# Weight tiles moved by 64 bytes in SBUF, to a multiple of 128 bytes, in a hybrid convolution and RWKV-7 block

## The chip, the cores and the metric

The kernel runs on one core of one Trainium2 chip. The metric is the device time of one execution in microseconds; the time shown is the median of three runs. A difference of 0.2% (some 6 us) is about what a measurement of this kernel can tell from no change.

## What is computed

One decoder block for 2,048 tokens and 1,024 channels, all in fp32. With `h = rmsnorm(x)·(1 + scale) + shift` the reference does, cut to what matters:

```python
p = jnp.einsum('bsd,de->bse', h, w_in[l])          # 1024 -> 73 tiles of 128 channels
c_val, c_gate, c_og, ts, r_og, g_conv, g_rwkv = jnp.split(p, SPLITS, axis=-1)
y_conv = _conv_branch(c_val, c_gate, c_og, ..., w_conv_out[l])   # depthwise conv 31, layernorm, swish, @ w_conv_out
y_rwkv = _rwkv7_branch(ts, r_og, ..., w_rwkv_out[l])             # delta-rule recurrence over time, @ w_rwkv_out
m = jax.nn.sigmoid(g_conv) * y_conv + jax.nn.sigmoid(g_rwkv) * y_rwkv
x = x + gate[:, None, :] * jnp.einsum('bsd,de->bse', m, w_out[l])
return _rmsnorm(x, final_g)
```

The four large products (`w_in`, `w_conv_out`, `w_rwkv_out`, `w_out`) hold nearly all of the arithmetic.

## The kernel before

**Products in three parts.** Each fp32 operand is split into a high part (type fp32r) and the rest, `hi` and `lo`, and a product is the sum of three: hi·hi, lo·hi, hi·lo. For `w_in` the weights are the stationary operand and the activations `h_hi`, `h_lo` the moving one. The tokens are worked off in four blocks of 512 (`TB`); a block's 512 columns are sent as two halves of 256 (`MS = 2`), and each half is a weight load and a matmul of its own:

```python
# L200-207, mm3k: one of the eight k of a product
for t, (ww, aa) in enumerate(((whi, ahi), (whi, alo), (wlo, ahi))):
    for q in range(ms):
        qs = slice(q * NS, q * NS + NS)
        nc.tensor.matmul(ps[:, qs], ww[:, k, :], aa[k][:, qs], ...)      # L206
```

So one product is 8·3·2 = 48 pairs of a weight load of 128 columns and a matmul of 256 columns.

**Two phases.** Phase 1 does, block by block, the 73 products with `w_in` (L206 with `h_hi`, `h_lo`), the convolution on VectorE (L774, one instruction for each of 30 further taps), and the recurrence in chunks of 64 tokens (L534 to L739). Phase 2 does the products with `w_rwkv_out` and `w_conv_out` (L206 with `MS2 = 1`, so matmuls of 512 columns; moving operands `o_*`, `u_*`, `m_*`) and with `w_out` (L1090 to L1092). In the last the roles are swapped: `m_hi`, `m_lo` (under the names `o_*` in blocks 0 and 2, `m_*` in blocks 1 and 3) are stationary and the weights move, 256 columns at a time.

**Weight tiles.** They come from one pool, `whl`, with seven slots (`WB = 7`) of 128 partitions by 4,096 bytes. `load_w` fetches a raw tile into a slot (`w_st`), ScalarE rounds it into a second (`w_hi`, L189), GpSimd or VectorE subtracts into a third (`w_lo`, L191), and for `w_in` both are written to DRAM, so that blocks 1 to 3 fetch the two halves ready made (L183, L186). All DMAs are issued in order by the SP queue; a load into a slot waits until the matmuls that read the slot's last tile are done. Two front products of block 0 keep their weights elsewhere, in tiles called `w_f`.

**Where tiles lie.** Pools opened without a side are stacked from the low end of SBUF, in the order in which they are opened: the constants `cst`, the weights `whl`, then `c1`, `l3`, `lt` (constants, state and chunk tiles of phase 1), in whose place phase 2 puts `b2` and `hl` (`y`, `u_*`, `m_*`). Pools opened with `side="right"` are stacked from the high end: `e1`, `xp`, `hp`, `e2` (among them `h_hi`, `h_lo`) and later `ob`, `f2`, `oa` (among them `o_*`). Each tile takes its bytes in a partition rounded up to 32. `cst` begins at byte 1,152 = 9·128 and holds

```
ident 512, v 580 -> 608, g_col 32, hgate_col 32, ghalf 64, shift_col 32, ones 512, hlg 32, hlb 32   = 1856 = 14*128 + 64
```

so the weight tiles begin at byte 3,008, and every one of the seven lies 64 bytes past a multiple of 128 (192 past a multiple of 256). Other places that matter below, as bytes past a multiple of 256: `h_*` 192, `o_*` 160, `m_*` and `u_*` 32, `w_f` 96, `th` and `yj` 128, `oc` and `vv` 96 or 224. From `xp`, `hp` and `e1` down to the smallest tile, what lies on the right is independent of the size of `cst`. Between the end of the left pools of phase 1 (byte 147,936) and the lowest tile that phase 2 opens on the right while these are still in use (`mr0`, byte 148,128) there are 192 bytes.

The instructions' order on each engine is worked out when the program is built, from a simulated timeline of the operations.

Of the kernel before, what the change touches and what calls it, by code (L numbers as in the profile page):

```python
# [9 lines left out]
F32 = mybir.dt.float32  # L10
# [8 lines left out]
P = 128  # L19
D = 1024  # L20
KT = D // P
# [60 lines left out]
def hybrid_block(ctx: ExitStack, tc: tile.TileContext, x, vecs, convk, w2a2, final_g, ada, w_in, w_co, w_ro, w_o, crow, out,  # L82
# [6 lines left out]
    cst = ctx.enter_context(tc.tile_pool(name="cst", bufs=1))  # L89
# [22 lines left out]
    def vc(name, j=None):  # L112
        o, w = VOFF[name]
        return v[:, o:o + w] if j is None else v[:, o + j:o + j + 1]
# [150 lines left out]
    nc.sync.dma_start(v, vecs)  # L265
    ab = vc("ada_b")
    hlg = cst.tile([P, KT], F32, name="hlg")
    hlb = cst.tile([P, KT], F32, name="hlb")
    nc.vector.tensor_scalar(out=hlg, in0=vc("conv_ln_g"), scalar1=0.5, scalar2=None, op0=ALU.mult)
    nc.vector.tensor_scalar(out=hlb, in0=vc("conv_ln_b"), scalar1=0.5, scalar2=None, op0=ALU.mult)  # L270

# [898 lines left out]
```

## Time and profile before

| | |
|---|---|
| time, median of 3 runs | 3031.91 us (3030.95 to 3034.19) |
| the profiled execution's own time | 3047.45 us |
| its span, first to last instruction | 3045.7 us |
| busy PE, weight loads (PEld), DVE, ACT, POOL | 96%, 90%, 68%, 31%, 41% |
| mean granted TensorE clock | 0.975 |
| moved by DMA | 699.24 MB, mean 230 GB/s |

The profile is one execution. PE is TensorE's matmuls, PEld its weight loads, DVE VectorE, ACT ScalarE, POOL GpSimd, SP the queue that issues the DMAs. A group of instructions is named by source line and by "out<-in" with the names of the tiles; for a matmul the first name behind the arrow is the moving operand and the second the stationary one. No view shows an address; the places above come from the allocation.

### The profile page before, as it was taken

What the parts mean: (1) busy time and instruction counts of PE and PEld (TensorE: products, weight loads), DVE (VectorE), ACT (ScalarE), POOL (GpSimd) and SP (SyncE); (2) the same over time, 40 slices, a digit from 0 to 9 for tenths busy, and PEclk for the clock granted to TensorE, in tenths of its full rate; (3) what the DMA queues carried; (4) which work ended last, traced back from release to release, by engine and by line L of the source; (5) the groups of instructions that cost most, each with busy time, mean ns of one, the idle gap of its engine ahead of it and who ended that gap; (6) DMA issues with size and microseconds to landing.
All of it is one profiled execution on the core that took longest, in us unless ns stands there. A gap on an engine that the chain in (4) does not pass through costs nothing.

```text
span 3045.7 us, 64763 instructions
## 1 busy us (share of the span) xinstructions
PE 2914.9 (96%) x25672; PEld 2735.9 (90%) x25672; DVE 2058.4 (68%) x3896; ACT 935.2 (31%) x1759; POOL 1250.1 (41%) x1786
## 2 busy tenths in 40 slices
PE   6999998999999999899999999999999999899998
PEld 6889998989989899899999999999999988788988
DVE  6587877686867676668676767676779635776433
ACT  4433434332323232233232323232323222333201
POOL 3455555434343425143434263625467204565000
PEclk9899999999999999999999999999999999999999
DMA  8666758564758578847474777655647778889674
GB/s 303 205 234 209 251 196 282 199 235 145 250 185 260 187 242 287 235 137 246 151 246 139 246 254 252 199 185 165 212 141 246 229 264 309 320 311 344 239 280 163
DMA packets 368673, 699.24 MB, mean 230 GB/s; under 512 B 136241, under 2 KB 154993, under 8 KB 368370
## 3 DMA queue, kind: packets, MB, share of 16 engines
q1 hardware_dynamic: 368370, 695.10, 68.0%
q8 instruction: 202, 3.31, 0.4%
q14 instruction: 101, 0.83, 0.1%
HBM read 506.14 MB, written 187.70 MB: 228 GB/s over the span
## 4 chain that ended last, share of the span: by engine, by line
PE 61%; DMA 16%; DVE 9%; POOL 7%; SPq 3%; issue 2%; ACT 2%; ACTq 0%; DVEq 0%; POOLq 0%
PE ps_main L206 43%; DMA w_st<-w_in_t 3%; PE aux L534 2%; POOL TT L627 2%; POOL itmp L625 2%; DMA w_st<-w_ro_t 2%; DMA w_st<-w_co_t 2%; PE pout L1091 2%; PE pout L1092 2%; PE pout L1090 2%; PE xo L689 2%; DVE acc L774 1%; DMA w_gr<-grow_d 1%; PE xo L684 1%; PE xo L695 1%
## 5 line engine op out<-in xcount | busy, mean ns | idle before, releaser
L206 PE MATMUL ps_main<-h_hi,w_hi 128*128 128x256 f32 x4608 | 971.3, 289 | 12.2 <-ACT w_hi L189 3.4
L206 PE MATMUL ps_main<-h_hi,w_lo 128*128 128x256 f32 x4608 | 965.4, 289 | 8.5 <-POOL w_lo L191 5.0
L206 PE MATMUL ps_main<-h_lo,w_hi 128*128 128x256 f32 x4608 | 971.3, 289 | 0.0
L206 PEld LDWEIGHTS ps_main<-h_hi,w_hi 128*128 128x128 f32 x4608 | 735.3, 194 | 24.1 <-ACT w_hi L189 3.9
L206 PEld LDWEIGHTS ps_main<-h_hi,w_lo 128*128 128x128 f32 x4608 | 731.8, 194 | 17.5 <-POOL w_lo L191 6.3
L206 PEld LDWEIGHTS ps_main<-h_lo,w_hi 128*128 128x128 f32 x4608 | 733.9, 194 | 8.1 <-issue 0.5
L774 DVE SCALAR_TENSOR_TENSOR acc<-u,ck,acc 128x512 f32<-128x512 f32 x928 | 698.6, 753 | 20.8
L625 POOL TENSOR_TENSOR itmp<-La,TT 128x126 f32<-128x126 f32 (+22 forms) x496 | 180.2, 363 | 140.9 <-DMA La<-dA 106.1
L627 POOL TENSOR_TENSOR TT<-TT,itmp 128x126 f32<-128x126 f32 (+22 forms) x496 | 188.2, 379 | 37.3
L681 ACT ACTIVATE Se<-S,pe 128x128 f32<-128x128 f32 x256 | 89.0, 395 | 239.4 <-DVE S L699 239.2
L191 POOL TENSOR_TENSOR w_lo<-w_st,w_hi 128x1024 fp32r<-128x1024 f32 x47 | 113.6, 2417 | 112.8 <-ACT w_hi L189 106.2
L699 DVE TENSOR_TENSOR S<-xo,Se 64x128 f32<-64x128 f32 x256 | 73.5, 287 | 104.1 <-PE xo L695 100.8
L189 ACT CAST w_hi<-w_st 128x1024 fp32r<-128x1024 f32 x71 | 74.2, 1046 | 182.4 <-DMA w_st<-w_in_t 147.4
L534 PE MATMUL aux<-KR,BK 64*128 64x128 f32 x1024 | 121.5, 307 | 7.4 <-POOL BK L517 4.1
L534 PEld LDWEIGHTS aux<-KR,BK 64*128 64x128 f32 x1024 | 104.2, 208 | 18.7 <-POOL BK L517 4.3
L562 POOL TENSOR_TENSOR BK<-BK,pe 128x1024 f32<-128x1024 f32 x32 | 62.0, 1939 | 140.7 <-PE aux L534 113.1
L691 DVE TENSOR_TENSOR uv<-xo,rn 64x256 f32<-64x256 f32 x128 | 53.8, 420 | 90.7 <-PE xo L689 88.8
L686 DVE TENSOR_TENSOR XO<-xo,XO 128x256 f32<-128x256 f32 x128 | 53.7, 420 | 89.9 <-PE xo L684 70.5
L537 DVE TENSOR_TENSOR As<-aux,maskA 128x512 f32<-128x512 f32 x128 | 83.8, 685 | 36.9 <-PE aux L534 35.6
L684 PE MATMUL xo<-S,KR 128*128 128x128 f32 x512 | 83.0, 285 | 15.0 <-DVE S L699 14.9
L786 ACT ACTIVATE th<-ps_main 128x512 f32<-128x512 f32 x64 | 38.1, 596 | 190.1 <-PE ps_main L206 168.9
L431 ACT ACTIVATE t<-ps_main,mu 128x512 f32<-128x512 f32 x96 | 65.6, 683 | 97.4 <-PE ps_main L206 90.4
(301 smaller groups left out, 5318.2 us busy)
## 6 DMA issues: line engine op xcount, KB each, us to landing
w_hi<-kh_in SPq DMA_DIRECT2D x219, 512.0 KB, 5.1
w_lo<-kl_in SPq DMA_DIRECT2D x219, 512.0 KB, 4.0
w_st<-w_in_t SPq DMA_DIRECT2D x73, 512.0 KB, 4.9
kh_in<-w_hi SPq DMA_DIRECT2D x71, 512.0 KB, 2.9
kl_in<-w_lo SPq DMA_DIRECT2D x71, 512.0 KB, 3.7
w_hi<-kh_ro SPq DMA_DIRECT2D x32, 512.0 KB, 5.6
w_lo<-kl_ro SPq DMA_DIRECT2D x32, 512.0 KB, 5.5
w_hi<-kh_co SPq DMA_DIRECT2D x32, 512.0 KB, 5.5
```

The costliest lines, as they stand in the source:

```text
L189: nc.scalar.copy(hi, st)
L191: lo_eng.tensor_tensor(out=lo, in0=st, in1=hi.bitcast(F32), op=ALU.subtract)
L206: nc.tensor.matmul(ps[:, qs], ww[:, k, :], aa[k][:, qs], start=(k == 0 and t == 0 and q == 0), stop=(k == KT - 1 and t == 2 and q == ms - ...
L431: nc.scalar.activation(t1, ps, AF.Identity, scale=mu1[:, mi:mi + 1])
L534: nc.tensor.matmul(pA[hh][:, c // 2, es], BK[hs, cc, es], KR[hs, cc, es], start=(c == 0), stop=(c == 3), skip_group_check=True)
L537: nc.vector.tensor_tensor(out=Asb[:, hh, c4 * 4:c4 * 4 + 4, :].rearrange("p (a e) n -> p a (e n)", e=2), in0=pA[hh], in1=flat(maskA).unsqu ...
L625: nc.gpsimd.tensor_tensor(out=tmp[:, :ni, :nt], in0=La[:, j:j + 1, j + 1:].broadcast_to([P, ni, nt]), in1=TT[:, :ni, j:j + 1].broadcast_to ...
L627: nc.gpsimd.tensor_tensor(out=TT[:, :ni, j + 1:], in0=TT[:, :ni, j + 1:], in1=tmp[:, :ni, :nt], op=ALU.add)
L681: nc.scalar.mul(Se[:, q, :], Sg[:, q, :], R[q]["pe"][:, c:c + 1])
L684: nc.tensor.matmul(xo[:, q, :], R[q]["KR"][:, cc, es], Sg[:, q, :], start=(q == 0), stop=(q == 1), skip_group_check=True)
L699: nc.vector.tensor_tensor(out=Sg[hs, :, hs], in0=xo[hs, 2:4, hs], in1=Se[hs, :, hs], op=ALU.add)
L774: nc.vector.scalar_tensor_tensor(out=acc if i + 1 < HALO else yj, in0=u[:, i:i + TB], scalar=ck[:, j, i:i + 1], in1=acc, op0=ALU.mult, op1 ...
```

## The change

```diff
     hlg = cst.tile([P, KT], F32, name="hlg")
-    hlb = cst.tile([P, KT], F32, name="hlb")
+    hlb = cst.tile([P, 24], F32, name="hlb")[:, :KT]
```

`hlb` (the halved bias of the convolution's layer norm) takes 96 bytes in a partition in place of 32; its first eight columns are used as before. `cst` is then 1,920 = 15·128 bytes, the weight tiles begin at byte 3,072 (a multiple of 128, 256 and 512), and everything stacked on them from the low end moves up by 64 bytes too. Nothing on the right moves. No instruction is added, removed or changed in its shape.

## The prediction

> **What bounds the kernel now.** I read the page's busy shares, slices and chain first, then the groups, then who waits for whom on PE and SP, and last the timeline, for the pace of the matmuls.
>
> ```profile
> span 3045.7 us, 64763 instructions
> PE 2914.9 (96%) x25672; PEld 2735.9 (90%) x25672; DVE 2058.4 (68%) x3896; ACT 935.2 (31%) x1759; POOL 1250.1 (41%) x1786
> ...
> PE   6999998999999999899999999999999999899998
> ...
> PE 61%; DMA 16%; DVE 9%; POOL 7%; SPq 3%; issue 2%; ACT 2%; ACTq 0%; DVEq 0%; POOLq 0%
> ...
> L206 PE MATMUL ps_main<-h_hi,w_hi 128*128 128x256 f32 x4608 | 971.3, 289 | 12.2 <-ACT w_hi L189 3.4
> L206 PE MATMUL ps_main<-h_hi,w_lo 128*128 128x256 f32 x4608 | 965.4, 289 | 8.5 <-POOL w_lo L191 5.0
> L206 PE MATMUL ps_main<-h_lo,w_hi 128*128 128x256 f32 x4608 | 971.3, 289 | 0.0
> L206 PEld LDWEIGHTS ps_main<-h_hi,w_hi 128*128 128x128 f32 x4608 | 735.3, 194 | 24.1 <-ACT w_hi L189 3.9
> ...
> L774 DVE SCALAR_TENSOR_TENSOR acc<-u,ck,acc 128x512 f32<-128x512 f32 x928 | 698.6, 753 | 20.8
> ...
> L191 POOL TENSOR_TENSOR w_lo<-w_st,w_hi 128x1024 fp32r<-128x1024 f32 x47 | 113.6, 2417 | 112.8 <-ACT w_hi L189 106.2
> ...
> L189 ACT CAST w_hi<-w_st 128x1024 fp32r<-128x1024 f32 x71 | 74.2, 1046 | 182.4 <-DMA w_st<-w_in_t 147.4
> ```
>
> PE is busy 96% of the span in almost every slice, and 61% of the chain is PE. In phase 1 alone there are 3 · 4,608 = 13,824 pairs of weight load and matmul. What others make PE wait for on account of weight tiles is small:
>
> ```profile
> PE ps_main L206 <- POOL w_lo L191: 5.0, 6, 1.4
> ...
> PE ps_main L206 <- DMA w_lo<-kl_in: 3.5, 3, 2.5
> ...
> PE ps_main L206 <- ACT w_hi L189: 3.4, 2, 2.3
> ...
> PE ps_main L206 <- DMA w_hi<-kh_in: 2.5, 1, 2.5
> ...
> PE pout L1091 <- DMA w_lo<-kl_o: 2.0, 1, 2.0
> ...
> SPq L183 <- PE ps_main L206: 717.8, 194, 10.8
> ```
>
> Loads of weights wait for PE to free a slot (717.8 us on SP), and PE hardly waits for loads (3.5 + 2.5 + 2.0 = 8.0 us). So the one price that decides is the pace of PE. A duration of 289 ns overlaps with the next, so the pace is read from counts in stretches of unbroken matmuls of 256 columns:
>
> ```profile
> 128.00:160.00 32.00, 32.00 (x269) 1.00 0.74 249
> ...
> 2856.00:2899.50 43.50, 43.50 (x375) 1.00 0.58 200
> 2718.00:2744.00 26.00, 26.00 (x221) 1.00 0.74 254
> ```
>
> The columns are the stretch, its length, PE's busy time with the count, the granted clock, the share of DMA. About two of each count only reach in over an edge. The first stretch is phase 1 (`h` moving, `w` stationary): 32.00 / 267 = 119.9 ns. The second is the last product of block 2 (`w` moving, `o` stationary): 43.50 / 373 = 116.6 ns. The third is that of block 1 (`w` moving, `m` stationary): 26.00 / 219 = 118.7 ns. With 120 ns, phase 1's pairs are 13,824 · 0.120 = 1,659 us, more than half of the span.
>
> **The change, part by part.** No instruction, DMA or wait is added or removed; addresses move. So there are only possible differences in the pace of what reads or writes the moved tiles.
>
> *PE, phase 1: weights stationary, from 64 to 0 past a multiple of 128.* The trace has a place where the same matmul takes its weights from elsewhere, the `w_f` tiles at 96 past a multiple of 256, next to rows of the ordinary slots at 192:
>
> ```profile
> 54.81 0.64 PE L206 MATMUL ps_f<-h_hi,w_f 128*128 128x256 f32 x4
> 55.29 0.40 PE L206 MATMUL ps_f<-h_lo,w_f 128*128 128x256 f32 x2
> 55.53 0.64 PE L206 MATMUL ps_f<-h_hi,w_f 128*128 128x256 f32 x4
> ...
> 128.07 0.40 PE L206 MATMUL ps_main<-h_hi,w_lo 128*128 128x256 f32 x2
> 128.31 0.40 PE L206 MATMUL ps_main<-h_hi,w_hi 128*128 128x256 f32 x2
> 128.55 0.40 PE L206 MATMUL ps_main<-h_lo,w_hi 128*128 128x256 f32 x2
> 128.79 0.40 PE L206 MATMUL ps_main<-h_hi,w_lo 128*128 128x256 f32 x2
> ```
>
> From 54.81 to 55.53 there are 4 + 2 matmuls in 0.72 us, 120 ns each; from 128.07 to 128.79 six in 0.72 us, 120 ns each. Weights that lie 96 bytes further back in their 256, not even on a multiple of 64, go at the same pace. That is the nearest row, and I take 0 from it. The ends: `m` against `o` as stationary operand are the same instructions with the same moving weights, and differ in where the operand lies (32 or 160 past a multiple of 256). They differ by 118.7 − 116.6 = 2.1 ns, so a place can cost that much. Upward I bound with 2.1 · 13,824 = +29 us. Downward the best pace that any 256-column matmul shows is 116.6 ns: (119.9 − 116.6) · 13,824 = −46 us.
>
> A rule of the Trainium skill bears on this: TensorE: Matmul & The Clock Gate, section "Step-by-step: what each phase is for", says that PE reads the moving and the stationary operand through two independent ports, and that loading the next weights takes no read bandwidth from the running matmul. By that rule a stationary operand's place could not matter and the sum would be 0; the 2.1 ns between `o` and `m` are not explained by it, so I keep both ends.
>
> *PE, phase 2.* In the products of 512 columns the weights are stationary too:
>
> ```profile
> 2804.75 50.40 PE ps_main L206 x216
> 2899.96 89.60 PE ps_main L206 x384
> ```
>
> 89.60 / 384 = 233.3 ns, just twice the 116.6 ns of the best 256-column rows, so nothing here is above the best pace; I take 0. In L1090 to L1092 (256 matmuls for each line and each of `o` and `m`, 1,536 in all) the weights move; `m` shifts with them and `o` does not, so the pair of `o` changes its distance and that of `m` keeps it. At 2.1 ns either way that is ±3 us; I take 0.
>
> *Transfers into and out of the weight tiles.* Of the issues from SBUF, `yj` and `th` lie at a multiple of 128 now, and `oc` and `vv` do not:
>
> ```profile
> w_hi<-kh_in SPq DMA_DIRECT2D x219, 512.0 KB, 5.1
> ...
> bv_d<-vv SPq DMA_DIRECT2D x32, 256.0 KB, 2.3
> co_d<-th SPq DMA_DIRECT2D x32, 256.0 KB, 3.6
> ...
> y_d<-yj SPq DMA_DIRECT2D x32, 256.0 KB, 3.6
> o_d<-oc SPq DMA_DIRECT2D x32, 256.0 KB, 4.6
> ```
>
> The aligned ones take 3.6 us to land, the others 2.3 and 4.6: the place does not order them. I take 0. If these loads became shorter, the 8.0 us for which PE waits on them are the most it could give; cover for the rest is PE's own stream, with seven slots. If they grew longer by a tenth (0.5 us of 5.1), each still lands within the 48 · 0.120 = 5.8 us of one product ahead, and the 8.0 us would grow by about 1 us.
>
> Against this stands a rule of the Trainium skill: DMA: Bandwidth & Descriptors, section "How a descriptor splits into AXI transactions", says that a transfer that does not start at a multiple of 256 bytes is charged for the whole first transaction. As an estimate from that page a row of 4,096 bytes at 192 past such a multiple takes 134 beats and would take 128 after the change, 4.5% less. The trace shows no such order in the rows above.
>
> *ScalarE, GpSimd and VectorE on weight tiles* (1,046 and 2,417 ns an instruction, 3.4 and 5.0 us of waiting on PE). VectorE's L774 reads `u` from 30 starts 4 bytes apart, which run over a multiple of 128 bytes once; single taps in a row:
>
> ```profile
> 211.09 0.74 DVE L774 SCALAR_TENSOR_TENSOR acc<-u,ck,acc 128x512 f32<-128x512 f32 x1
> ...
> 212.41 0.74 DVE L774 SCALAR_TENSOR_TENSOR acc<-u,ck,acc 128x512 f32<-128x512 f32 x1
> ...
> 213.48 0.74 DVE L774 SCALAR_TENSOR_TENSOR acc<-u,ck,acc 128x512 f32<-128x512 f32 x1
> ```
>
> All are 0.74 us beside the mean of 753 ns over 928, so a start does not show there. For the others I take 0; were they slower by a tenth, the 8.4 us of waits would gain some 1 us. The recurrence's tiles on the left move from 96 to 160 or from 224 to 32 past a multiple of 256, so none becomes aligned: 0.
>
> **Sum:** 0. The profiled execution would again be about 3047.5 us, 0.5% above the median of the runs shown (3031.9), so the time is 3,032 us. By steps without PE's pace the spread is −8 to +5 us.
>
> **The rivals.** *A, faster: phase 1 is held back by the weights' place.* Counted from the moving to the stationary operand, within 256 bytes, `h` and `w` are 0 apart now and 64 after; `w` and `o` are 224 apart and run 3.3 ns faster. If reads that are in step disturb each other, moving `w` alone takes them out of step. Against it: `h` and `w_f`, 160 apart, go at 120 ns. Price: −46 us on PE; 43% of the span is L206 on the chain (the line below), about 1,310 us, of which 1,536 · 0.233 = 358 us are phase 2, so at least (1,310 − 358) / 1,659 = 57% of it counts, −26 us, and as PE is busy all along rather more: −40, that is 2,992 us.
>
> ```profile
> PE ps_main L206 43%; DMA w_st<-w_in_t 3%; PE aux L534 2%; POOL TT L627 2%; POOL itmp L625 2%; DMA w_st<-w_ro_t 2%; DMA w_st<-w_co_t 2%; PE pout L1091 2%; PE pout L1092 2%; PE pout L1090 2%; PE xo L689 2%; DVE acc L774 1%; DMA w_gr<-grow_d 1%; PE xo L684 1%; PE xo L695 1%
> ```
>
> *B, slower: the new place of the weights is the bad one.* The pair `w` and `m`, 96 apart and so nearest to the new 64, shows the extra 2.1 ns over `o`. If that adds to phase 1's 120 ns, PE takes 29 us more, most of it on the end: +25, that is 3,057 us. It decides from 0.45 ns a matmul on (6 us / 13,824). For it: the size of the effect is seen. Against it: again `w_f`, whose other place changes nothing.
>
> *C, faster: the transfers gain, by the alignment rule.* Not over the 8.0 us of waits on PE, and by a 4.5% share of them only 0.4 us; to show, nearly all waits would have to go: 3,025 us.
>
> *D, the program is ordered otherwise.* An order that depends on addresses, or a left tile that now meets a right one, would move instructions. 64 bytes more leave 128 of the 192 free bytes, and the shapes that the order is worked out from are the same, so I give it little, either way.
>
> **How the numbers follow.** No change 0.50 (own range 3,026 to 3,038, the ±0.2%); A 0.30; C 0.02; B 0.14; D 0.04, half each way. So faster 0.34, same 0.50, slower 0.16. The forecast is the likeliest, 3,032. The range reaches down to the bound of A, 3,032 − 46 = 2,986, and up to 3,052, within B, which leaves out some 0.1 above and little below.
>
> **What would show it.** Right: unbroken stretches of L206 at 120 ns, the same 13,824 pairs, PE's busy time within 6 us of 2914.9, the waits on weight tiles still near 16 us. A shows as a pace below 119.5 ns in phase 1 and PE's busy time down by up to 46 us; B as a pace above 120.5. C shows as shorter landings of `w_hi<-kh_in` (5.1 us) at an unchanged pace; D as other counts or another order. The prediction is wrong if phase 1's pace changes at all, since no other step holds 6 us.

## The result

The changed kernel takes 3012.68 us (median, 3010.32 to 3017.85) against 3032.32 us before (3030.95 to 3034.19): a ratio of 0.9928, 95% interval 0.991 to 0.9946, so 19.6 us faster, three times the smallest difference that a measurement here can tell from nothing. A second set of runs (`after_again`) gave 0.9912 (0.9896 to 0.9929). No change was forecast; the gain is the one that rival A named, at half its size (19.6 us in place of 40).

The page after, its busy line and the first two lines of the chain:

```profile
span 3008.6 us, 64763 instructions
PE 2853.2 (95%) x25672; PEld 2675.1 (89%) x25672; DVE 2060.3 (68%) x3896; ACT 935.1 (31%) x1759; POOL 1254.4 (42%) x1786
...
PE 43%; DMA 20%; DVE 14%; POOL 11%; issue 5%; SPq 4%; ACT 3%; POOLq 0%; ACTq 0%; DVEq 0%
PE ps_main L206 31%; POOL TT L627 4%; POOL itmp L625 4%; DMA w_st<-w_in_t 3%; DVE acc L774 3%; DMA w_gr<-grow_d 2%; DMA w_st<-w_ro_t 2%; DMA w_st<-w_co_t 2%; PE aux L534 2%; PE pout L1091 1%; PE pout L1092 1%; PE pout L1090 1%; DMA La<-dA 1%; PE xo L689 1%; DMA dT<-TT 1%
...
L206 PE MATMUL ps_main<-h_hi,w_hi 128*128 128x256 f32 x4608 | 950.9, 285 | 16.6 <-DVE u L767 3.8
L206 PE MATMUL ps_main<-h_hi,w_lo 128*128 128x256 f32 x4608 | 944.6, 284 | 7.3 <-DMA w_lo<-kl_in 3.7
L206 PE MATMUL ps_main<-h_lo,w_hi 128*128 128x256 f32 x4608 | 951.1, 285 | 0.0
```

The counts are those of before, and so is the order of the instructions on every engine, line by line. The other engines' busy times are the same within 0.4%. PE alone is shorter, 2914.9 to 2853.2, by 61.7 us, and its share of the chain falls from 61% to 43%: more of the chain of this execution is now work of others that PE waits for. The share is no exact measure, since an execution at the pace of before can have 54% (`both_moved`, below).

The pace of phase 1 has changed, and it takes two values. The same unbroken stretches of L206 in the chain in order of time (start, length, what), first before, then after:

```profile
2096.23 24.67 PE ps_main L206 x204
2391.87 22.99 PE ps_main L206 x190
```

```profile
2061.50 24.22 PE ps_main L206 x204
2354.23 21.75 PE ps_main L206 x190
```

Less the last matmul's own 0.29 us, the x204 stretch goes at 24.38 / 203 = 120.1 ns before and 117.9 after, the x190 at 22.70 / 189 = 120.1 and 113.5. Over all stretches of twelve matmuls without a break phase 1's pace was 119.9 ns and is 114.9: in some 58% of them near 113.3 and in 33% near 117.8. The granted clock is 1.00 in the four stretches above, so the clock does not make the difference. A product stays in the one or the other until the stream is broken by a wait or other work, and after the break it can go on at the other; the slot that the weights lie in does not decide it, since by the allocation the same pair of slots shows both.

Two further groups fit no rule of alignment. `w_f`, whose place went from 96 to 160 past a multiple of 256 (a multiple of 32 as before), is faster; and L1090 with `o`, whose moving weights have become aligned, is slower. The timeline and the stretch of L1090 to L1092 in block 2, after (columns as in the prediction):

```profile
54.79 0.63 PE L206 MATMUL ps_f<-h_hi,w_f 128*128 128x256 f32 x4
...
56.19 0.63 PE L206 MATMUL ps_f<-h_hi,w_f 128*128 128x256 f32 x4
```

```profile
2818.00:2860.00 42.00, 42.00 (x352) 1.00 0.55 193
```

From 54.79 to 56.19 twelve matmuls (four and two, twice) take 1.40 us, 116.7 ns in place of 120; the second, with the two that reach in over an edge left out, is 42.00 / 350 = 120.0 ns in place of 116.6. What both have in common is the distance. Counted from the moving to the stationary operand within 256 bytes, `h` to `w_f` went from 160 to 224 and `w` to `o` from 224 to 160: the two have changed places, and so have their paces. That gave the theory for the experiments: the pace follows from how far the two operands of PE lie apart, modulo 256 bytes (the remainder after division by 256), and not from where the weights lie.

### The profile page after: what moved, and what is told of

Read it like the earlier page. It is cut to its first block, busy times and chain, and to the rows that moved or that the text cites. A ratio compares the mean times of both kernels' runs of the same rounds, so it can differ in the third digit from the quotient of the medians.

```text
span 3008.6 us, 64763 instructions
## 1 busy us (share of the span) xinstructions
PE 2853.2 (95%) x25672; PEld 2675.1 (89%) x25672; DVE 2060.3 (68%) x3896; ACT 935.1 (31%) x1759; POOL 1254.4 (42%) x1786
## 4 chain that ended last, share of the span: by engine, by line
PE 43%; DMA 20%; DVE 14%; POOL 11%; issue 5%; SPq 4%; ACT 3%; POOLq 0%; ACTq 0%; DVEq 0%
PE ps_main L206 31%; POOL TT L627 4%; POOL itmp L625 4%; DMA w_st<-w_in_t 3%; DVE acc L774 3%; DMA w_gr<-grow_d 2%; DMA w_st<-w_ro_t 2%; DMA w_st<-w_co_t 2%; PE aux L534 2%; PE pout L1091 1%; PE pout L1092 1%; PE pout L1090 1%; DMA La<-dA 1%; PE xo L689 1%; DMA dT<-TT 1%
## 5 line engine op out<-in xcount | busy, mean ns | idle before, releaser
L206 PE MATMUL ps_main<-h_hi,w_hi 128*128 128x256 f32 x4608 | 950.9, 285 | 16.6 <-DVE u L767 3.8
L206 PE MATMUL ps_main<-h_hi,w_lo 128*128 128x256 f32 x4608 | 944.6, 284 | 7.3 <-DMA w_lo<-kl_in 3.7
L206 PE MATMUL ps_main<-h_lo,w_hi 128*128 128x256 f32 x4608 | 951.1, 285 | 0.0
L206 PEld LDWEIGHTS ps_main<-h_hi,w_hi 128*128 128x128 f32 x4608 | 718.7, 191 | 29.2 <-ACT w_hi L189 4.2
L206 PEld LDWEIGHTS ps_main<-h_hi,w_lo 128*128 128x128 f32 x4608 | 714.8, 191 | 15.8 <-POOL w_lo L191 4.7
L206 PEld LDWEIGHTS ps_main<-h_lo,w_hi 128*128 128x128 f32 x4608 | 717.4, 191 | 8.1 <-issue 0.4
L534 PE MATMUL aux<-KR,BK 64*128 64x128 f32 x1024 | 115.3, 296 | 5.8 <-POOL TT L620 2.2
L689 PE MATMUL xo<-XO,As 64*64 64x64 f32 x1024 | 91.1, 228 | 8.7 <-DVE XO L686 8.7
L689 PEld LDWEIGHTS xo<-XO,As 64*64 64x64 f32 x1024 | 71.3, 136 | 29.0 <-DVE XO L686 10.2
```

What stands on the lines that cost most here:

```text
L206: nc.tensor.matmul(ps[:, qs], ww[:, k, :], aa[k][:, qs], start=(k == 0 and t == 0 and q == 0), stop=(k == KT - 1 and t == 2 and q == ms - ...
L534: nc.tensor.matmul(pA[hh][:, c // 2, es], BK[hs, cc, es], KR[hs, cc, es], start=(c == 0), stop=(c == 3), skip_group_check=True)
L689: nc.tensor.matmul(xo[pr_, q, hs], As[q][pr_, hh, c, kcol(e)], XO[pr_, c, q, hs], start=(q == 0 and hh == 0), stop=(q == 1 and hh == 1), s ...
```

## The experiments

Rivals to that distance theory: the alignment theory (it is the weights' own multiple of 128 that helps) and the transfer theory (loads and stores of aligned tiles help).

**Both operands moved.** The change, and `h` moved down by 192 bytes through a longer tile in front of it on its side, so that the distance is 0 again with all weights at a multiple of 256. The tiles of `xp` and `e2`, which lie behind, move with `h` here and in every run that lengthens `lw`; none of them is an operand of L206 in phase 1.

```diff
-        lw = e1.tile([P, TB], F32R, name="lw", tag="lw")
+        lw = e1.tile([P, TB + 48], F32R, name="lw", tag="lw")[:, :TB]
```

> The change as it is, and h_hi, h_lo moved down by 192 bytes as well, so that weights and h both begin at a multiple of 256 and lie 0 apart again, as before. Distance theory (PE's pace depends on how far the stationary operand lies from the moving one, counted within 256 bytes): unbroken L206 of phase 1 at 120 ns as before the change, PE busy near 2915 us, 3032 us, the same as before within 0.2%. Alignment theory (the weights' own place at a multiple of 128 is what helps): pace of the changed kernel, 113 to 118 ns, PE busy near 2853 us, about 3013 us. Transfer theory (loads and stores of aligned weight tiles help): about 3013 us with the pace at 120 ns.

Measured: 1.0007 of the time before (0.9995 to 1.002), pace 119.9 ns throughout:

```profile
2085.40 24.67 PE ps_main L206 x204
2380.43 22.99 PE ps_main L206 x190
```

The rows are those of before to the hundredth. With the weights and their transfers aligned and only the distance undone, the whole gain is gone. That is against the alignment theory and the transfer theory both.

**`h` moved and the weights not.** The kernel before with `TB + 16` in the same line (64 bytes), `hlb` as before.

> The kernel before, weights still 64 past a multiple of 128, and only h_hi, h_lo moved down by 64 bytes, so that the weights lie 64 after h within 256 bytes, as in the changed kernel. Distance theory: L206 of phase 1 at 113 to 118 ns, L1090 to L1092 as before the change (116.7 with o, 118.5 with m), PE busy near 2850 us, 3010 to 3013 us, 0.6 to 0.8% faster than before. Alignment theory and transfer theory: 120 ns and 3032 us, no change.

Measured: 3007.86 us, 0.9914 (0.9895 to 0.9933), phase 1 at 114.7 ns on average with the same two paces, and L1090 to L1092 with `o` at 40.00 / 343 = 116.6 ns as before the change (second fence, columns as in the prediction):

```profile
2059.12 24.23 PE ps_main L206 x204
2351.83 21.75 PE ps_main L206 x190
```

```profile
2818.00:2858.00 40.00, 40.00 (x345) 1.00 0.56 197
```

The gain is had without any weight tile at a multiple of 128. Together with `both_moved` this shows the distance to be the cause of the gain, and not the place of either operand alone.

**Other distances.** `hlb` of 160 and of 224 bytes (`[P, 40]` and `[P, 56]`), then `h` moved by 224, 256 and 32 bytes with `hlb` as before (`TB + 56`, `TB + 64`, `TB + 8`).

> hlb takes 160 bytes in place of 32, weights and all that is stacked on them move by 128: the weights lie 64 past a multiple of 128 as before, and 128 after h within 256. Alignment and transfer theory: 120 ns, 3032 us. Distance theory: a pace other than 120 ns in phase 1; no distance of 128 has been seen, its neighbours are 118.5 at 96 and 120 at 160, so between 113 and 120 ns and 2995 to 3032 us; L1090 with o, now 96 from the weights, goes to 118.5 ns, and w_f, at 32, is new.

> hlb takes 224 bytes in place of 32: the weights begin at 128 past a multiple of 256, so at a multiple of 128 as in the changed kernel, but 192 after h within 256 instead of 64. Alignment theory (multiple of 128): the changed kernel's pace of 113 to 118 ns and 3013 us. Transfer theory with 256 as the unit: 3032 us at 120 ns. Distance theory: the pace of the distance 192, which lies between 160 (120 ns) and 224 (116.7 ns): 116 to 120 ns, 3005 to 3032 us; L1090 with o goes to the pace of distance 32, which is new.

> The kernel before with h_hi, h_lo moved down by 224 bytes: the weights, still 64 past a multiple of 128, lie 224 after h within 256. Distance theory: the pace that h with w_f after the change and w with o before it show at 224, 116.7 ns, steady: 13,824 times 3.2 ns is 44 us less of PE and, at the share of PE's gain that came through so far (20 to 26 us of 62 to 72), some 15 us, 3017 us. If instead only the distance of 64 is good: 120 ns and 3032 us.

> The kernel before with h_hi, h_lo moved down by 256 bytes. Distance theory with a period of 256 bytes: 120 ns as before, PE busy near 2915 us. With a period of 512 or more, or if the places of the two count one by one: another pace.

> The kernel before with h_hi, h_lo moved down by 32 bytes: the weights lie 32 after h within 256. Distance theory: as w_f with h in w_plus128 and o with w in w_plus192 at the same distance, 118.3 ns. If only a multiple of 64 between the two helps: 120 ns.

The same two stretches, one fence for each kernel, in this order: distances 128, 192, 224, 256 and 32.

```profile
2079.42 24.40 PE ps_main L206 x204
2376.21 22.75 PE ps_main L206 x190
```

```profile
2075.94 24.23 PE ps_main L206 x204
2368.89 21.74 PE ps_main L206 x190
```

```profile
2082.00 24.00 PE ps_main L206 x204
2378.82 22.37 PE ps_main L206 x190
```

```profile
2074.00 24.67 PE ps_main L206 x204
2371.03 22.99 PE ps_main L206 x190
```

```profile
2079.02 24.34 PE ps_main L206 x204
2371.45 22.68 PE ps_main L206 x190
```

Together (pace of phase 1 over all unbroken stretches of twelve; time as a ratio with its interval, where the kernel was timed):

| distance of `w` from `h` | pace, ns | time against before |
|---|---|---|
| 0 (before; both moved) | 119.9 | 1; 1.0007 (0.9995 to 1.002) |
| 32 | 118.3 | not told by one run, 3026.3 us |
| 64 (the change; `h` moved) | 114.9; 114.7 | 0.9928 (0.991 to 0.9946); 0.9914 (0.9895 to 0.9933) |
| 128 | 118.8 | 0.9988 (0.9971 to 1.0006) |
| 192 | 117.4, of it 9% near 113.3 | 0.9959 (0.9947 to 0.9971) |
| 224 | 117.1 | 0.9964 (0.9943 to 0.9985) |
| 256 | 119.9 | not told by one run, 3026.9 us |

At 256 the rows of before come back and at 128 they do not, so as far as these distances go the period is 256 bytes. At 192 the weights lie at a multiple of 128 as in the change, and the gain is half as large and comes at another pace: a multiple of 128 is not what counts. At 128 the alignment is that of before and the pace is another. The paces that other pairs had shown at 32 and 224 (118.3 and 116.7) hold for `h` and `w` within 0.4 ns; at 128 and 192 the values are new. At 224 the gain is 8.5 us where some 15 were expected, and the pace is not steady as expected: 63% of the stretches go near 116.7 ns and 36% near 117.8. The order of the times is that of the paces, but for 192 and 224, whose intervals overlap. The distance is not all: `w` to `m`, always 96 apart, went at 118.5 ns in most kernels but at 117.3 where both had moved by 128, and half at 117.5 and half at 120 where both had moved by 192.

**Matmuls of 512 columns.** `h_moved` with `MS = 1`.

> h_moved (weights 64 after h) with phase 1 in matmuls of 512 columns in place of two of 256, so half the weight loads there, 6,912. In all kernels so far matmuls of 512 columns run at 233.3 ns, twice 116.7, at distances 32, 96 and 160. If the distance counts through the weight loads that run beside a matmul, 512 columns stay at 233.3 ns at 64 too: 6,912 times 233.3 is 1,613 us against 13,824 times 114.7, 1,585, so slower than h_moved by some 10 to 28 us, 3018 to 3036. If it counts through the moving stream alone: 2 times 113.3, 226.7 ns, 1,567 us, and up to 18 us faster than h_moved, 2990 to 3008.

Measured: 3344.98 us, 1.1011 (1.0978 to 1.1044), far outside both expectations. The build ordered the work of phase 1 otherwise, PE's busy time rose to 2984.8 us, its idle time to 363 and the mean granted clock fell to 0.927, so the time says nothing of the distance. The pace does; two stretches of the chain in block 1:

```profile
1474.38 5.60 PE ps_main L206 x24
1510.20 5.14 PE ps_main L206 x22
```

5.60 / 24 and 5.14 / 22 are 233 ns: at 64 bytes the 512-column matmul runs at twice 116.7, as at the other distances seen, and not at twice 113.3, which is 226.7. So the distance counts where a weight load goes with every 256 columns and not where it goes with every 512. That speaks for the two reads of PE disturbing each other, which no run shows directly.

**Where the rest of the gain goes.** In the two profiled executions PE's own time fell by 61.7 us and the span by 37.1. The one before was a long execution, though; by the medians the kernel gained 19.6 us and, in the second set, 29.1. PE's saving is no fixed number either: at the paces of before its busy time was 2914.9, 2911.8 (`both_moved`) and 2898.1 us (`h_d256`), with the change 2853.2 and 2850.4 (`after_again`), so 45 to 65 us. Some 30 to 65% of it comes through. PE's waits (in total, times, longest), before and after:

```profile
PE xo L684 <- DVE S L699: 14.9, 12, 2.4
...
PE xo L689 <- DVE XO L686: 5.0, 5, 2.3
...
PE late L739 <- POOL XO L734: 3.4, 2, 1.8
```

```profile
PE xo L684 <- DVE S L699: 20.8, 15, 3.6
...
PE late L739 <- POOL XO L734: 9.8, 7, 2.1
PE xo L689 <- DVE XO L686: 8.7, 7, 2.5
```

They grew where the recurrence hands results back and forth (by 16.0 us in these three rows); PE's idle time went from 130.8 to 155.4 us. Between the recurrence's steps PE has a fixed number of other matmuls to do, and when these are shorter it comes to the next step early. One theory was that VectorE is late there because of the convolution's taps. Two kernels with 20 of the 30 taps left out, without and with the change:

```diff
-        for i in range(HALO):
+        for i in range(2, HALO, 3):
```

> The kernel before with 20 of the 30 further taps of the convolution left out (L774 at every third tap), some 450 us of VectorE's 698 us on that line; the weights lie 0 from h. Both theories: pace 120 ns; the order of the work is another, so its time is only the base for taps10_d64, somewhere between 2900 and 3030 us.

> taps10_d0 with the change (weights 64 after h). Theory that the missing two thirds of PE's gain went into waits on VectorE, whose queue is full of taps when the recurrence needs it: with few taps the gain comes through, 45 to 65 us against taps10_d0 in place of 20 to 26. Rival (it is lost in waits on other work, or in the clock): again some 20 to 26 us.

Measured: 3053.52 us (1.0086, 1.0066 to 1.0105) and 3035.8 us (1.0025, 1.0013 to 1.0036): the change brings 17.7 us, no more than with all taps, and the base is slower than expected. The theory fell. VectorE is busy only 54% there, and PE waits for other steps, some of them still VectorE's. The busy line and PE's waits, without and with the change:

```profile
PE 2899.8 (95%) x25672; PEld 2724.7 (89%) x25672; DVE 1632.9 (54%) x3256; ACT 936.2 (31%) x1759; POOL 1254.7 (41%) x1786
...
PE late L657 <- DVE T L653: 21.8, 17, 2.5
...
PE ps_main L206 <- DMA w_lo<-kl_in: 10.6, 4, 4.7
...
PE late L739 <- POOL XO L734: 8.7, 7, 2.7
```

```profile
PE 2854.8 (94%) x25672; PEld 2677.9 (88%) x25672; DVE 1635.9 (54%) x3256; ACT 935.6 (31%) x1759; POOL 1250.3 (41%) x1786
...
PE late L657 <- DVE T L653: 25.1, 18, 3.3
...
PE late L739 <- POOL XO L734: 16.1, 11, 3.1
PE ps_main L206 <- DMA w_lo<-kl_in: 13.9, 5, 5.0
```

So what comes through does not hang on the taps: with few of them PE's busy time falls by 45.0 us (2899.8 to 2854.8) and 17.7 come through, 39%. That it is the fixed order of other matmuls and recurrence steps is argued, not shown. The clock, which the expectation names as a rival, has a part that is not settled: the mean granted clock over all runs was 0.9768 without and 0.9718 with the change here, and 0.9798 and 0.9765 with all taps (`after_again` and the kernel before on its chip). As an estimate, the missing share of the clock times the run's time, that is 15 and 10 us more of lost PE time at the most. Whether the clock is lower because PE waits more often, no run shows.

**The two ways side by side.**

> The change itself on this chip, as the base for h_moved_again: 0.991 to 0.995 of the time before, 113.3 and 117.8 ns in phase 1.

> The kernel before with h moved in place of the weights. Distance theory: phase 1 as in the changed kernel, and L1090 to L1092 with o at 116.7 in place of 120 ns, 768 times 3.3 ns = 2.5 us less, so 1 to 5 us below after_again, which these rounds can hardly tell from nothing.

Measured on one chip: 0.9912 (0.9896 to 0.9929) and 0.9934 (0.9916 to 0.9952), that is 3000.05 and 3008.62 us. `h_moved_again` was to be 1 to 5 us below and is 8.6 above. The intervals overlap, and in the first sets the order was the reverse (0.9928 and 0.9914), so the runs do not tell the two apart. No version run here is shown to beat the changed kernel.

## Why the prediction was wrong

- **The step that failed** is the zero for PE in phase 1, taken from its nearest row. `w_f` against the ordinary slots, 120 ns each, was read as "the place of the stationary operand does not matter". It only says that distances 0 and 160 happen to be equally slow. One equal pair out of a period of eight steps of 32 bytes was taken for a rule, against the pair `m` and `o`, which showed a difference. In place of the zero, phase 1's pace fell from 119.9 to 114.9 ns over its 13,824 matmuls, because the weights came to lie 64 bytes from `h` in place of 0 (`both_moved` and `h_moved`).
- **The bounds of that step** were off too. The best 256-column pace of the trace, 116.6 ns, was taken as the lower end; at 64 the matmuls reach 113.3. By the pace that is (119.9 − 114.9) · 13,824 = 69 us, and PE's busy time fell by 61.7 us in the profiled pair, where 46 was the bound.
- **Rival A** counted the right thing, the distance between the two operands. That reads in step disturb each other is not shown, and `w_f` at 160, as slow as 0, does not fit it simply. Its time of 2,992 us was 21 us too low, since it let 40 of 46 us (87%) reach the end and some 30 to 65% did. That the measured time lies within the range is luck in part: the gain on PE was taken too small and the share that comes through too large.
- **Rival B** chose the wrong neighbour: the pace at 64 is not that of 96.
- **The rule of the two read ports** in the Trainium skill, TensorE: Matmul & The Clock Gate, section "Step-by-step: what each phase is for", would have given no effect of the place. The paces of 113 to 120 ns at equal instructions do not agree with it, if it is the weight load that slows the running matmul, which no run shows directly.
- **Transfers** were rightly put at zero. In `both_moved` all weight rows start at a multiple of 256 and the time is that of before; `w_hi<-kh_in` lands in 5.1 us before and after. The Trainium skill, DMA: Bandwidth & Descriptors, section "How a descriptor splits into AXI transactions", charges aligned rows less; nothing of that reaches the end here.
- **The rest held**: no count and no order changed (rival D), L1090 to L1092 moved by 3.3 ns with `o` (768 matmuls, 2.5 us, within the ±3 us) and by nothing with `m`, the 512-column products stayed at 233 ns, and VectorE's and the other engines' busy times stayed.
- The profile before was one of the longer executions: 3047.5 us, where later runs of the same kernel lie between 3016 and 3046. The difference of the two spans (37 us) overstates the gain for that reason.

## What to carry to other kernels

Where PE streams without a break, compare the pace of equal matmuls on operands from different places before assuming that an address costs nothing; if they differ, tabulate the pace against the distance between the moving and the stationary operand modulo 256 bytes, and move one of them by a few dozen bytes. One equal pair proves no independence, since the effect has a period and equal values within it. A gain on the busiest engine in a program with a fixed order can come through only in part: here some 30 to 65%.

## What was not expected of the hardware

The pace of a 256-column fp32r matmul with a weight load each ran from 113.3 to 120 ns with the same instructions in the same order, at a granted clock of 1.00, when tiles were moved so that the distance of its two operands modulo 256 bytes changed. At a distance of 64 it has two steady paces, 113.3 and 117.8 ns, held until the stream breaks; at 192 and 224 two show as well. What picks the one or the other is open. At 512 columns the pace was 233 to 234 ns at every distance seen (32, 64, 96, 160 and 224).
